# The eight sample rows of a decoder layer: weight rows taken four blocks at a time instead of two, with new numbers for the planner

## The chip, the cores and the metric

The kernel runs on one core of a Trainium2 chip. The metric is the device time of one execution in microseconds; the median of the runs is given. TensorE (PE) multiplies, VectorE (DVE) and ScalarE (ACT) work element by element, GpSimd (POOL) does small work and issues the DMAs that add to their target, and SyncE (SP) issues nearly all other DMAs.

## The reference

One layer of a decoder, all in float32, for 1024 rows of a prompt and 8 sample rows (one new position for each of 8 sequences). Cut to what matters here:

```
xn = rmsnorm(h) * pre_g
u, v, z_a, x_b, z_b, g_a, g_b = split(xn @ w_in)          # 7 x 1024 columns
y_a = gelu(u) * spatial_mix(layernorm(gelu(v))) * silu(z_a)
y_b = pool_branch(x_b) * silu(z_b)
m   = sigmoid(g_a) * (y_a @ w_pa) + sigmoid(g_b) * (y_b @ w_pb)
h   = h + rmsnorm(m @ w_out) * post_g                      # "out"
e   = p @ w_ple
h   = h + rmsnorm(sigmoid(rmsnorm(h) @ w_pg) * e)          # "gate"
```

Outputs are h for prompt and sample, and the new rows of two caches. The change concerns out and gate, the last two products with 1024 x 1024 weights.

## The kernel before

The work runs in stages, one for each product: embedding and x (to 66 us), v, the gate logits, u and z_a, x_b and z_b, y_a and y_b times their weights (to about 804), out (798 to 886) and gate (886 to 970), then the last norm and stores. Out and gate work on four pairs of 128-row blocks of the prompt. For each pair a Strassen scheme makes seven products (named by the weights they use: B11, B21, B22, T1 to T4); each is twelve matmuls of 128 x 512, since every float32 operand is split into a high and a low part (h and l in the names) and three of the four part products are taken. A product lands in PSUM (`acct`), and ScalarE and VectorE add it into the result.

The 8 sample rows are too few for that. In `sample_steps` (L934) their product goes the other way: the 8 rows, transposed (128 x 8), are the stationary operand, and rows of the weights stream past. A *load* brings two blocks of 128 weight rows (512 KB each; tile `worow` for out, `wgrow` for gate) and a *run* calls `sample_round` (L903), which makes four matmuls into four groups of 32 PSUM partitions of one bank (`sps`). Eight blocks make four rounds for each stage. After the last one `sample_sums` adds the groups, and the sample goes on as the prompt does: `out_finish(S)` (norm, then an adding DMA of 32 KB that puts the input row on `hs`), `gate_norm(S)` (`hn`) and `gate_input(S)` (its transposition through `psst`).

What sets the order: nothing is issued when the code is read. `Planner.take` records each operation with a reckoned duration. TensorE's products form a list of steps, and `at(step, ...)` hangs other work on a step; `OS` and `GS` are the steps in out's list (`oflow`) and gate's (`gflow`) at which Sample's rounds begin, and `TURNS` gives for each pair of the prompt the steps of `out_finish`, `gate_norm` and `gate_input`. `wanted` then works out from the end when each operation is due, and `order` deals out the engines' time by it: `LEAD` is how long before its due time an operation may go, `PATIENCE` (and `HASTE` inside `hasty`) how long after its recorded time it may be passed over, `lands` how long a DMA is reckoned to need after its bytes have moved. The result is one fixed order for each engine and for each DMA queue. All is issued from one line, L369, so the profile is read by the names of tiles.

Of the kernel before, what the change touches and what calls it, by code (L numbers as in the profile page):

```python
# [16 lines left out]
NB = D // P  # L17
# [3 lines left out]
HALF = 512  # L21
# [3 lines left out]
QT = WIDE // 2  # L25
EPS = 1e-6
POOL_BUF = 15
FAST = (1, 1, 0, 1)
SIDES = (0, 1, 0, 1, 0, 0, 0, 0)
EARLY = 40.0  # L30
WE = 2
PUSH = {'norm': -5.0, 'half': 0.0, 'cut': 0.0, 'e': -4.0, 'we': -4.0, 'vw': -5.0, 'p': -1.0}
WARM = 8
HASTE = 8.0
TURNS = ((7, 8, 11), (14, 14, 18), (21, 26, 28), (30, 33, 35))
OS, GS = 5, 12
WINDOWS = (2, 4, 8, 16)
PLE = 256
SLOTS = 46
# [55 lines left out]
class Planner:  # L95
# [5 lines left out]

    SEEN = {"tensor": 0.25, "vector": 0.15, "scalar": 0.20, "gpsimd": 0.20}
    TABLES = {AF.Gelu_apprx_tanh: 1, AF.Sigmoid: 2, AF.Silu: 3}
    LOAD, LEAD, PATIENCE, RATE, SPARE = 14.98, 14.0, 55.8, 0.36, 3
    SPARED = 1.0

    def __init__(self, nc, slots, queues):
# [98 lines left out]
    def take(self, engine, method, args, kwargs):  # L206
        given = [*(("out" if i == 0 else "", a) for i, a in enumerate(args)), *kwargs.items()]
        writes = [a for k, a in given if k in ("out", "accum_out") and a is not None]
        reads = [a for k, a in given if k not in ("out", "accum_out") and hasattr(a, "tensor")]
        if kwargs.get("accum_op") is not None:  # L210
            reads += writes
        name = writes[0].tensor.name
        if engine == "tensor" and self.open is not None and self.open[0] == name:
            op = self.open[1]
        else:
            op = Op(engine, len(self.ops), self.clock, self.fixed)
            op.patience, op.push = self.patience, self.push
            self.ops.append(op)
        self.open = (name, op) if engine == "tensor" else None
        op.calls.append((method, args, kwargs))  # L220
        op.spent.append(op.busy)
        if method == "dma_start":
            run = min(self.run(a) for a in (writes[0], reads[0]))
            op.busy, op.moved = 1.0 if engine == "gpsimd" else 0.45, writes[0].size() * 4e-6 * (1 + 0.2 / run)
            op.lands = 2.0
            if kwargs.get("accum_op") is not None:
                op.moved, op.lands = 2 * op.moved, 3.5
        else:
            took = self.duration(engine, method, writes[0], reads, kwargs)
            op.busy += took  # L230
            if engine == "tensor" and not self.fixed:
                self.clock += took
            if engine == "scalar":
                op.table = self.TABLES.get(kwargs["func"], 0)
        for ap in reads:
            self.touch(op, ap, False)
        for ap in writes:
            self.touch(op, ap, True)
# [138 lines left out]
def hybrid_step(  # L377
# [14 lines left out]
    plan = Planner(nc, SLOTS, {"acc": 3, "bank": 2})  # L392
# [8 lines left out]
    def slot(name, shape=(P, T), dt=F32):  # L401
        n_name[0] += 1
        name, n = f"{name}_{n_name[0]}", 1
        for d in shape[1:]:
            n *= d
        model = big.rearrange("p b t -> p (b t)")[:, :n].bitcast(dt)
        if len(shape) > 2:
            dims = "abc"[: len(shape) - 1]
            model = model.rearrange(f"p ({' '.join(dims)}) -> p {' '.join(dims)}", **dict(zip(dims, shape[1:])))
        return plan.slot(name, model, lambda i: spool.tile(list(shape), dt, tag=f"slot{i}", name=name, bufs=1))  # L410
# [21 lines left out]
    def dma(out, in_, by=None):  # L432
        (by or nc.sync).dma_start(out=out, in_=in_)
# [14 lines left out]
    nc.gpsimd.memset(mhalf, -0.5)  # L448
    rc = cpool.tile([P, POOL_BUF], F32, tag="rc", name="rc")
    for j in range(POOL_BUF):  # L450
        nc.gpsimd.memset(rc[:, j : j + 1], 1.0 / (j + 1))
# [42 lines left out]
    class Operand:  # L494
# [37 lines left out]
        def at(self, what, k):  # L532
            return [part[:, k % 2, :] for part in self.parts[what, k // 2]]

    class Stored(Operand):


        ROWS = {"B11": ("b", 0, 0), "B21": ("b", 1, 0), "B22": ("b", 1, 1), "T2": ("low", 0, 0),
                "T1": ("low", 0, 1), "T4": ("high", 0, 0), "T3": ("high", 0, 1)}
# [360 lines left out]
                nc.tensor.matmul(ps, hi(k), wl, start=False, stop=False)  # L900
                nc.tensor.matmul(ps, lo(k), wh, start=False, stop=k == w.nk - 1)

    def sample_round(ps, turned, weights, r):  # L903

        plan.apart()
        for q in range(4):
            k, j = r + q // 2, q % 2
            nc.tensor.matmul(ps[32 * q : 32 * q + NS, :], turned[k], weights(k, j),
                             start=r == 0, stop=r == len(turned) - 2)
# [24 lines left out]
    def sample_steps(key, src, steps, turned, finish):  # L934
        rows, ps = {}, []

        def load(r):
            for k in (r, r + 1):
                t = rows[k] = slot(f"{key}row", (P, D))
                dma(t, src[k * P : (k + 1) * P, :])  # L940

        def run(r):
            if not ps:
                ps.append(bank("sps"))
            sample_round(ps[0], turned(), lambda k, j: rows[k][:, j * HALF : (j + 1) * HALF], r)
            if r == NB - 2:
                finish(ps[0])

        for i, r in enumerate(range(0, NB, 2)):
            at(steps[2 * i], lambda r=r: load(r))  # L950
            at(steps[2 * i + 2], lambda r=r: run(r))


    roots = {}
# [64 lines left out]
    turned = dram.tile([SEQ, D], F32, tag="vturned", name="vturned")  # L1019
# [57 lines left out]
    def early_loads():  # L1077
        lnt["w00"] = cpool.tile([P, NB], F32, tag="w00", name="w00")
        dma(lnt["w00"], w_s[:, 0, 0].partition_broadcast(P))
        dma(o_spool[0, :, : POOL_BUF - 1, :], state[:, 1:, :])  # L1080

# [150 lines left out]
    def pool_state():  # L1232
        dma(big[: NS * POOL_BUF, 7, :D], state.rearrange("b r d -> (b r) d"))

    def small_tables():

        for g, w in enumerate(WINDOWS):
            m = masks[g] = small.tile([P, NS], F32, tag="mask", name=f"mask{g}", bufs=NPAIR)
            nc.gpsimd.memset(m, 1.0)
            nc.gpsimd.affine_select(out=m, in_=m, pattern=[[-POOL_BUF, NS]], compare_op=ALU.is_ge,  # L1240
                                    fill=0.0, base=w - 1 - POOL_BUF, channel_multiplier=1)
            nc.gpsimd.affine_select(out=m, in_=m, pattern=[[POOL_BUF, NS]], compare_op=ALU.is_ge,
# [152 lines left out]
    steps = [s for p in vsteps + gasteps for s in p] + every(usteps)  # L1395
# [24 lines left out]
    for n, t in enumerate([NB - 1, *range(NB - 1)]):  # L1420
        s = 5 + 4 * n
# [51 lines left out]
    rows = lambda t: NS if t == S else P  # L1473
# [93 lines left out]
    def hasty(do, ts):  # L1567
        plan.patience = HASTE
        for t in ts:
            do(t)  # L1570
        plan.patience = plan.PATIENCE
# [102 lines left out]
    for i in range(NPAIR):  # L1674
        ts = [2 * i + 1, 2 * i]
        for do, s in zip((out_finish, gate_norm, gate_input), TURNS[i]):
            at((oflow + gflow)[s], lambda do=do, ts=ts: hasty(do, ts))
# [71 lines left out]
    def begin():  # L1749
# [37 lines left out]
        embed(0, 0)  # L1787
        pushed("e", embed_out, 0, 0, FAST[0])
        embed(1, 0)
        pushed("e", embed_out, 1, 0, FAST[1])  # L1790
        vps = bank("vecs")
# [3 lines left out]
        embed(0, 1)  # L1795
        pushed("e", embed_out, 0, 1, FAST[2])
        pushed("half", x_half, 0, (0, 1))
        pushed("cut", xop.cut, "B11")
        pushed("vw", steps[0].prepare)
        embed(1, 1)  # L1800
        pushed("e", embed_out, 1, 1, FAST[3])
        pushed("half", x_half, 0, (2, 3))
# [73 lines left out]
```

## Time and profile before

| | us |
|---|---|
| runs shown: median (lowest to highest of 3) | 981.69 (978.53 to 984.54) |
| the profiled execution: time | 979.92 |
| its span | 978.2 |
| TensorE busy | 965.4 (99% of the span) |
| VectorE busy | 805.7 (82%) |
| ScalarE busy | 495.5 (51%) |
| granted TensorE clock | 0.997 |

A row of the timeline gives start and duration in us, the engine, the operation, output <- inputs by their names, sizes, and in brackets how long the engine had stood idle and who released it. A row of a tile gives durations in ns (lowest, median, highest) and the first and last start. A matmul in float32 takes two passes and leaves two records, so the four matmuls of a round are eight records. Ends of matmuls are modelled; what counts is the distance of their starts. A row of windows has, behind its stretch and length, the busy time and count of PE, PEld (TensorE's loading of weights), DVE, ACT and POOL in turn, the clock, the share of the DMA engines and GB/s.

### The profile page before, as it was taken

To read this page: it belongs to the slowest core of one execution; us is meant where nothing else is said; L and a number is where in the kernel's file an instruction comes from. 1 tells how busy PE (TensorE), PEld (TensorE's weight loads), DVE (VectorE), ACT (ScalarE), POOL (GpSimd) and SP (SyncE) were. 2 spreads that over 40 slices of the span, in tenths; PEclk is the share of its full clock that TensorE was granted. 3 is DMA by queue.
4 is the path that set the end of the run, shared out by engine and by line. 5 is a ranking of instruction groups with operands and counts; after the bars stand their busy time and mean duration, and the time that the engine had idled before them with its cause. 6 is when DMAs were issued, how large, how long until landed. Compare 5 with 4: busy or idle time off the path is not lost. (4 is left out here: it accounts for less than half of the span.)

```text
span 978.2 us, 15914 instructions
## 1 busy us (share of the span) xinstructions
PE 965.4 (99%) x6048; PEld 858.1 (88%) x6048; DVE 805.7 (82%) x1251; ACT 495.5 (51%) x847; POOL 72.8 (7%) x117
## 2 busy tenths in 40 slices
PE   9999999999999999999999999999999999999996
PEld 7889999999999998999999999999999997778775
DVE  7798568978879789887777897698699899779987
ACT  7674346767434544242423343463363273688655
POOL 2200000000000000000010100000000001323212
PEclk9999999999999999999999999999999999999998
DMA  9464654423457787541222266692592385698996
GB/s 347 148 151 88 152 135 148 162 95 116 171 213 275 257 281 238 188 153 54 87 76 93 75 218 244 222 376 91 170 370 87 120 306 177 160 300 296 222 326 209
DMA packets 128505, 185.81 MB, mean 190 GB/s; under 512 B 42150, under 2 KB 85198, under 8 KB 128421
## 3 DMA queue, kind: packets, MB, share of 16 engines
q1 hardware_dynamic: 126093, 176.91, 54.4%
q0 software_dynamic: 2048, 7.37, 4.2%
q8 instruction: 47, 0.77, 0.3%
q10 hardware_dynamic: 288, 0.52, 0.2%
q14 instruction: 29, 0.24, 0.1%
HBM read 129.27 MB, written 55.96 MB: 189 GB/s over the span
## 5 line engine op out<-in xcount | busy, mean ns | idle before, releaser
L369 DVE TENSOR_TENSOR u<-acc,u 128x520 f32<-128x520 f32 (+1 forms) x90 | 62.5, 695 | 29.8 <-PE acc L369 29.8
L369 POOL TENSOR_TENSOR rstd<-ms,mhalf 128x1 f32<-128x1 f32 (+1 forms) x37 | 30.1, 840 | 448.7 <-DVE ms L369 448.0
L369 ACT ACTIVATE u<-acc 128x512 f32<-128x512 f32 x39 | 23.2, 596 | 35.0 <-PE acc L369 32.5
L369 ACT ACTIVATE zbw<-zbs 128x512 fp32r<-128x512 f32 x16 | 10.0, 629 | 31.6 <-DVE zbs L369 25.8
L369 DVE TENSOR_TENSOR big<-big 128x1024 f32<-128x1024 f32 (+4 forms) x20 | 24.7, 1262 | 0.1
L369 POOL COPY big<-xb 128x1 f32<-128x1 f32 x8 | 3.5, 443 | 260.9 <-ACT xb L369 218.0
L369 ACT ACTIVATE big<-mix 128x256 f32<-128x256 f32 x32 | 11.9, 382 | 20.6 <-PE mix L369 19.7
L369 ACT ACTIVATE paw<-pas 128x512 fp32r<-128x512 f32 x16 | 10.1, 630 | 24.0 <-DVE pas L369 20.0
L369 ACT ACTIVATE pbw<-pbs 128x512 fp32r<-128x512 f32 x16 | 10.1, 630 | 22.3 <-DVE pbs L369 17.0
L369 PE MATMUL accm<-qh,wpoolw 128*128 128x260 f32 (+1 forms) x96 | 21.0, 320 | 0.0
L369 DVE TENSOR_TENSOR zbw<-zbs,zbw 128x512 fp32r<-128x512 f32 x16 | 10.9, 689 | 12.0 <-ACT zbw L369 11.9
L369 ACT ACTIVATE gbw<-gbs 128x512 fp32r<-128x512 f32 x16 | 10.1, 630 | 20.9 <-DVE gbs L369 11.7
L369 ACT ACT_TABLE_LOAD x11 | 14.1, 1283 | 7.4 <-PE acc L369 3.6
L369 ACT ACTIVATE junk<-h 128x512 bf16<-128x512 f32 x25 | 15.7, 627 | 3.5 <-DVE h L369 3.0
L369 DVE SCALAR_TENSOR_TENSOR zb<-accm,gvec,zb 128x512 f32<-128x512 f32 (+1 forms) x16 | 12.0, 750 | 6.5 <-PE accm L369 6.4
L369 PEld LDWEIGHTS accm<-qh,wpoolw 128*128 128x128 f32 x96 | 15.6, 189 | 1.9
L369 ACT ACTIVATE u<-acct 128x512 f32<-128x512 f32 x22 | 13.0, 590 | 7.4 <-PE acct L369 5.1
L369 DVE TENSOR_TENSOR paw<-pas,paw 128x512 fp32r<-128x512 f32 x16 | 10.9, 687 | 6.7 <-ACT paw L369 6.7
L369 ACT ACTIVATE mw<-ms 128x512 fp32r<-128x512 f32 x16 | 10.0, 625 | 12.4 <-DVE ms L369 9.7
L369 ACT ACTIVATE xbw<-xbs 128x512 fp32r<-128x512 f32 x16 | 10.0, 626 | 11.7 <-DVE xbs L369 10.0
L369 PE MATMUL mix<-wst,vh 128*128 128x256 f32 x64 | 15.6, 321 | 0.0
L369 ACT ACTIVATE uw<-us 128x512 fp32r<-128x512 f32 x16 | 10.0, 625 | 10.0 <-DVE us L369 5.9
(660 smaller groups left out, 3557.7 us busy)
## 6 DMA issues: line engine op xcount, KB each, us to landing
ga<-ga SPq DMA_DIRECT2D x16, 516.0 KB, 5.9
gb<-gb SPq DMA_DIRECT2D x16, 516.0 KB, 7.2
ya<-za SPq DMA_DIRECT2D x8, 516.0 KB, 4.9
yb<-zb SPq DMA_DIRECT2D x8, 516.0 KB, 2.6
x<-in_x_prompt_dram SPq DMA_DIRECT2D x8, 512.0 KB, 7.3
vraw<-in_w_in_dram SPq DMA_DIRECT2D x8, 512.0 KB, 5.9
e<-e SPq DMA_DIRECT2D x8, 512.0 KB, 5.9
vturned<-v SPq DMA_DIRECT2D x32, 128.0 KB, 3.4
```

Source lines behind the costliest of these rows:

```text
L369: getattr(getattr(self.nc, e), method)(*(self.real(a) for a in args), **{k: self.real(a) for k, a in kwargs.items()})
```

## The change

`ROWS = 4`: a load takes four blocks and a run makes two rounds one after the other, as one piece that the planner can't part. There are two loads and two runs for each stage in place of four and four. Out's runs hang on steps 5 and 9 of `oflow` in place of 7, 9, 11 and 13, gate's on 16 and 20 of `gflow` in place of 14, 16, 18 and 20. With `OS` the sample's `out_finish`, `gate_norm` and `gate_input` come two steps sooner. `TURNS` changes for the first two pairs: `gate_input` of the first goes from step 11 to 8, `gate_norm` of the second from 14 to 17. An adding DMA of under 0.3 MB, of which there is one, `hs`, is reckoned to land in 7.0 us instead of 3.5. `HASTE`, `LEAD` and `PATIENCE` change slightly.

```diff
+ROWS = 4
-HASTE = 8.0
-TURNS = ((7, 8, 11), (14, 14, 18), (21, 26, 28), (30, 33, 35))
-OS, GS = 5, 12
+HASTE = 7.8
+TURNS = ((7, 8, 8), (14, 17, 18), (21, 26, 28), (30, 33, 35))
+OS, GS = 3, 14
...
-    LOAD, LEAD, PATIENCE, RATE, SPARE = 14.98, 14.0, 55.8, 0.36, 3
+    LOAD, LEAD, PATIENCE, RATE, SPARE = 14.98, 13.58, 51.894, 0.36, 3
...
-                op.moved, op.lands = 2 * op.moved, 3.5
+                op.moved, op.lands = 2 * op.moved, 3.5 if op.moved > 0.3 else 7.0
...
-    def sample_round(ps, turned, weights, r):
-        plan.apart()
+    def sample_round(ps, turned, weights, r, apart=True):
+        if apart:
+            plan.apart()
...
-            for k in (r, r + 1):
+            for k in range(r, r + ROWS):
...
-            sample_round(ps[0], turned(), lambda k, j: rows[k][:, j * HALF : (j + 1) * HALF], r)
-            if r == NB - 2:
+            at_once = turned()
+            for s in range(r, r + ROWS, 2):
+                sample_round(ps[0], at_once, lambda k, j: rows[k][:, j * HALF : (j + 1) * HALF], s, s == r)
+            if r == NB - ROWS:
                 finish(ps[0])
-        for i, r in enumerate(range(0, NB, 2)):
-            at(steps[2 * i], lambda r=r: load(r))
-            at(steps[2 * i + 2], lambda r=r: run(r))
+        for i, r in enumerate(range(0, NB, ROWS)):
+            at(steps[ROWS * i], lambda r=r: load(r))
+            at(steps[ROWS * i + 2], lambda r=r: run(r))
```

The change moves instructions on all engines. Three places on which the prediction rests:

TensorE in out, around Sample's first run; `mw` is the prompt's operand, `big` holds the sample rows. Before:

```order
L369 MATMUL acct_491<-woB22l_8784,mw_8780 128x512
L369 MATMUL acct_491<-woB22h_8724,mw_8780 128x512
L369 MATMUL sps_497<-worow_8709,big 8x512 x2
L369 MATMUL sps_497<-worow_8713,big 8x512 x2
L369 MATMUL acct_502<-woT2h_8546,mw_8814 128x512
L369 MATMUL acct_502<-woT2l_8598,mw_8814 128x512
```

With the change:

```order
L370 MATMUL acct_491<-woT1h_8696,mw_8710 128x512
L370 MATMUL sps_494<-worow_8650,big 8x512 x2
L370 MATMUL sps_494<-worow_8654,big 8x512 x2
L370 MATMUL sps_494<-worow_8661,big 8x512 x2
L370 MATMUL sps_494<-worow_8669,big 8x512 x2
L370 MATMUL acct_491<-woB22h_8715,mw_8786 128x512
L370 MATMUL acct_491<-woB22l_8800,mw_8786 128x512
```

Two rounds stand in a row, and ahead of products (B22, then B11) that in before came ahead of the first round. TensorE's order up to out is the same as in before.

VectorE in the stage of x_b and z_b, near 378 us; `za` is copied out of PSUM (`acc`) in two pieces, `big` is the layer norm of v. Before:

```order
L369 TENSOR_TENSOR xbw_4437<-xbraw_4374,xbw_4437 128x512
L369 TENSOR_TENSOR za_4457<-acc_354,u_4305 128x512
L369 TENSOR_TENSOR xbw_4451<-xbs_4440,xbw_4451 128x512
L369 TENSOR_TENSOR za_4457<-acc_355,u_4305 128x520
L369 SCALAR_TENSOR_TENSOR big<-big,lncol,off_2206 128x8x128 x2
L369 TENSOR_TENSOR za_4457<-za_4457,u_4244 128x1032
```

With the change:

```order
L370 TENSOR_TENSOR xbw_4437<-xbraw_4374,xbw_4437 128x512
L370 SCALAR_TENSOR_TENSOR big<-big,lncol,off_2206 128x8x128
L370 TENSOR_TENSOR xbw_4457<-xbs_4440,xbw_4457 128x512
L370 TENSOR_TENSOR za_4484<-acc_355,u_4305 128x520
L370 TENSOR_TENSOR za_4484<-acc_354,u_4305 128x512
L370 SCALAR_TENSOR_TENSOR big<-big,lncol,off_2206 128x8x128
L370 TENSOR_TENSOR xbw_4451<-xbs_4433,xbw_4451 128x512
```

One of the two instructions on `big` now stands ahead of the 520-wide `za`, and the 512-wide one behind it.

VectorE at the very end of gate, the last norms of the last pair (`ge`; the multiplication by `rstd` is each row's last step before its store). Before:

```order
L369 TENSOR_SCALAR sofar_638<-ssq_635,sofar_636 128x1
L369 TENSOR_TENSOR ge_10078<-ge_10078,out_9456 128x256
L369 SCALAR_TENSOR_TENSOR ge_10058<-ge_10058,rstd_634,hback_10053 128x512
L369 TENSOR_SCALAR ms_639<-ssq_637,sofar_638 128x1
L369 TENSOR_TENSOR ge_10078<-ge_10078,out_9456 128x256
L369 SCALAR_TENSOR_TENSOR ge_10058<-ge_10058,rstd_634,hback_10053 128x512
L369 SCALAR_TENSOR_TENSOR ge_10078<-ge_10078,rstd_640,hback_10060 128x512 x2
```

With the change:

```order
L370 TENSOR_SCALAR ms_633<-ssq_631,sofar_632 128x1
L370 TENSOR_TENSOR ge_10056<-ge_10056,out_9460 128x512
L370 TENSOR_SCALAR sofar_638<-ssq_635,sofar_636 128x1
L370 TENSOR_TENSOR ge_10077<-ge_10077,out_9460 128x256
L370 TENSOR_SCALAR ms_639<-ssq_637,sofar_638 128x1
L370 TENSOR_TENSOR ge_10077<-ge_10077,out_9460 128x256
L370 SCALAR_TENSOR_TENSOR ge_10056<-ge_10056,rstd_634,hback_10051 128x512 x2
L370 SCALAR_TENSOR_TENSOR ge_10077<-ge_10077,rstd_640,hback_10058 128x512 x2
```

The four final multiplications stand together at the end; in before one of them came ahead of `ms_639`. On ScalarE the wide sum of squares that `ms_633` needs now stands behind both 256-wide pieces of `ge`, in before between them.

## The prediction

> **What bounds the kernel now.** I read the page first, then the waits of PE, then the stretches around each edit.
>
> ```profile
> span 978.2 us, 15914 instructions
> PE 965.4 (99%) x6048; PEld 858.1 (88%) x6048; DVE 805.7 (82%) x1251; ACT 495.5 (51%) x847; POOL 72.8 (7%) x117
> ```
>
> TensorE is busy for 99% of the span. A change can only shorten what TensorE executes, remove one of its few stalls, or alter what follows its last matmul. These are the stalls inside the run (time waited, number, longest):
>
> ```profile
> PE acct L369 <- ACT h L369: 1.2, 1, 1.2
> PE acc L369 <- DVE za L369: 0.7, 1, 0.7
> PE acct L369 <- ACT ge L369: 0.6, 1, 0.6
> ```
>
> There is about 3 us to win from stalls, and about as much to lose wherever something is now late. So each term below is around 1 us, against a time of 980. All terms are differences against the profiled execution: 979.92 us, span 978.2.
>
> **Merged rounds.** The change removes no matmul: Sample's rows are still multiplied in eight rounds, four in out and four in gate, eight records each. It removes boundaries between these rounds and the products of 128 columns. One round of before, in TensorE's timeline:
>
> ```profile
> 925.14 0.40 PE L369 MATMUL acct<-wgB11h,hw 128*128 128x512 f32 x1
> ...
> 927.70 0.40 PE L369 MATMUL acct<-wgB11h,hw 128*128 128x512 f32 x1
> 928.03 1.04 PE L369 MATMUL sps<-wgrow,sst 128*8 128x512 f32 x8
> 929.00 0.50 PE L369 MATMUL acct<-wgT2h,hw 128*128 128x512 f32 x1
> 929.34 0.40 PE L369 MATMUL acct<-wgT2l,hw 128*128 128x512 f32 x1
> ```
>
> From 925.14 to 927.70 stand eleven steps of a product, 0.233 us each, so a product of twelve takes 2.8. From 927.70 to 929.34 the round costs 1.64 − 2 × 0.233 = 1.18 us. Inside a round the four column groups run together and each takes two passes. The first and the last start of the four out rounds give the distance of the passes:
>
> ```profile
> L369 PE MATMUL sps<-worow,big x32: 592/594/597, 823.7 to 844.3; 128*8 128x512 f32 x32
> 843.87 1.04 PE L369 MATMUL sps<-worow,big 128*8 128x512 f32 x8
> 844.84 0.50 PE L369 MATMUL acct<-woB11h,mw 128*128 128x512 f32 x1
> ```
>
> The last round starts at 843.87 and its last record at 844.3: 0.43 a pass. A second round straight behind the first should add two passes, 0.87 us, instead of 1.18, a gain of 0.31. There are four such merges (two in out, two in gate): **−1.2 us**. No row shows two rounds back to back. The low bound is no gain, if the second round waits for the first as a product does; the high one is 4 × (1.18 − 0.59), each second round costing one record's length: −2.4. I take the pass distance, the nearest row.
>
> The Trainium skill (TensorEngine Tiling (Array Packing), Key Properties) says that changing the tiling mode drains TensorE, while changing only the tile does not. The trace agrees that the change of mode costs: 927.70 to 928.03 is 0.33 and 929.00 to 929.34 is 0.34, each 0.10 over a step. By that rule alone the eight crossings saved are worth 0.8 us and the sum below would be 0.4 higher.
>
> **The stall at 864.** TensorE stands still once in out:
>
> ```profile
> 864.17 0.39 PE L369 MATMUL acct<-woT4h,mw 128*128 128x512 f32 x1
> 865.74 0.50 PE L369 MATMUL acct<-woB11h,mw 128*128 128x512 f32 x1 [1.18 <-ACT h L369]
> ```
>
> 1.57 less a step is 1.34 us lost. ScalarE was late, for this reason (its timeline, then the group of tile hs):
>
> ```profile
> 862.67 1.06 ACT L369 ACTIVATE hn<-hs 8x1024 f32<-8x1024 f32 x1 [1.73 <-DMA hs<-in_x_sample_dram]
> ...
> 865.10 0.59 ACT L369 ACTIVATE h<-acct 128x512 f32<-128x512 f32 x1
> ```
> ```profile
> L369 ACT ACTIVATE hs<-sps x1: 588/588/588, 846.7 to 846.7; 8x512 f32<-8x512 f32 x1
> ...
> L369 POOL DMA_DIRECT2D hs<-in_x_sample_dram x1: 851/851/851, 856.3 to 856.3; - x1
> ...
> DMA to landing us min/median/max: 6.3/6.3/6.3
> ```
>
> Behind hn stand a junk on h, a junk on acct and the h copy that frees the PSUM of the next product, 865.10 + 0.59. The adding load took 6.3 us where the planner reckoned 3.5; it now reckons 7.0. The new steps matter more. The first group of rounds now follows directly on T1, two products earlier than 823.7, so at 818.1. Four products later, at 818.1 + 2 × 1.02 + 4 × 2.8 = 831.3, comes the second, which ends near 833.4 instead of 844.84. Everything behind it (hs 846.7, the load 856.3, the landing 862.6) moves some 11 us forward: landing near 851. The transposition of hn on TensorE moves forward about ten, and keeps some 2 us behind hn. So the wait goes: **−1.3 us**; bounds 0 (another wait of the same size) and −1.3. The loads for the first group carry no waits on engines and landed from 808 to 816 in before; I cost them at nothing, covered by the product of T1.
>
> **A wait that grows, at 378.** Planner's numbers also move instructions far from Sample. At one place VectorE sets TensorE's next product:
>
> ```profile
> 375.18 0.69 DVE L369 TENSOR_TENSOR xbs<-xbraw,xbraw 128x512 f32<-128x512 f32 x1 [1.89 <-DMA xbraw<-in_w_in_dram]
> ...
> 377.12 0.68 DVE L369 TENSOR_TENSOR za<-acc,u 128x512 f32<-128x512 f32 x1
> 377.72 0.68 DVE L369 TENSOR_TENSOR xbw<-xbs,xbw 128x512 fp32r<-128x512 f32 x1
> 378.32 0.69 DVE L369 TENSOR_TENSOR za<-acc,u 128x520 f32<-128x520 f32 x1
> 378.93 2.47 DVE L369 SCALAR_TENSOR_TENSOR big<-big,lncol,off 128x1024 f32<-128x1024 f32 x2
> ```
> ```profile
> 377.93 0.39 PE L369 MATMUL acc<-xB11h,xbw 128*128 128x512 f32 x1
> 379.06 0.51 PE L369 MATMUL acc<-xB22h,zaw 128*128 128x260 f32 x2 [0.75 <-DVE za L369]
> ```
>
> TensorE starts at 379.06, when the 520-wide za ends (378.32 + 0.69). The order after puts one of the two big instructions (2.47 / 2 = 1.2) ahead of it and the 512-wide za (0.6) behind it. VectorE cannot start sooner, since the xbraw load releases it at 375.18. So za ends, and TensorE starts, 0.6 later: **+0.6 us**, bounds 0 (if that load lands earlier) and +1.2.
>
> **The gate stage.** The four wgrow loads of the first group now stand ahead of the transposing hblocks loads in SP's queue; in before two of them did. Another block's hblocks, which stood there too, go out earlier in return. What hangs on it:
>
> ```profile
> 916.56 3.04 SPq L369 DMA_DIRECT2D hblocks<-h  x4
> ```
> ```profile
> hblocks<-h SPq DMA_DIRECT2D x4, 128.0 KB, 10.1
> ```
> ```profile
> 929.88 1.24 DVE L369 STREAM_TRANSPOSE big<-hblocks 128x1024 f32<-128x1024 f32 x1
> 931.05 0.65 DVE L369 TENSOR_TENSOR hw<-hs,hw 128x512 fp32r<-128x512 f32 x1
> ```
> ```profile
> 932.33 0.63 PE L369 MATMUL acct<-wgT3h,hw 128*128 128x512 f32 x2
> ```
>
> The issues end at 919.6 and the loads take some 10 us to land, so the last is there near 929.1; VectorE needs 2.6 us more (hw ready at 931.7), 0.6 before its use. After, this product comes 3.1 us sooner: 1.3 and 0.6 from out, and one round of 1.2 that stood before it. So the wait begins with a landing after 926.6. The queue ahead has four hblocks less (512 KB in small pieces) and two wgrow more (1 MB in large ones), which I take to be about as long, and starts some 2 us sooner: landing near 927, a wait of **+0.4 us**. Bounds: 0, and rival (b).
>
> The new TURNS record the same norms and transposing loads of the prompt at other steps (gate_input of the first pair three steps sooner, gate_norm of the second three later). They add no instruction; I cost them at nothing, covered by the time in which VectorE idles before 868, and rival (a) is what they cost without that cover.
>
> **The tail.** After the last matmul, in before:
>
> ```profile
> 968.70 0.63 ACT L369 ACTIVATE junk<-ge 128x512 bf16<-128x512 f32 x1 [0.34 <-DVE ge L369]
> ...
> 969.46 0.21 DVE L369 TENSOR_SCALAR ms<-ssq,sofar 128x1 f32<-128x1 f32 x1 [0.52 <-ACT junk L369]
> ...
> 969.78 0.47 ACT L369 ACTIVATE ge<-acct,hscales 128x256 f32<-128x256 f32 x1 [0.36 <-PE acct L369]
> ...
> 972.12 0.66 POOL L369 TENSOR_TENSOR rstd<-ms,mhalf 128x1 f32<-128x1 f32 x1 [1.44 <-DVE ms L369]
> 972.28 2.07 DVE L369 SCALAR_TENSOR_TENSOR ge<-ge,rstd,hback 128x512 f32<-128x512 f32 x3
> ```
>
> The wide junk ran while ScalarE waited for the last product. In the new order it follows both 256-wide ge, so it starts at 970.25, and ms behind it near 971.1. All four final multiplies (2.07 / 3 = 0.69 each) then stand in a row at the end; before, one of them was done by 971.9. They start near 972.6 and end at 972.6 + 2.7 = 975.3, against 974.35: **+0.95 us**, bounds +0.4 (one multiply hidden in POOL's delay) and +1.5.
>
> **Sum.** −1.2 − 1.3 + 0.6 + 0.4 + 0.95 = −0.55, or 979.4 us for the profiled execution. The runs shown have a median of 981.69, 1.77 above it, so I forecast **981.1 us**: no change that can be measured (1%, or 9.8 us, is about what a measurement of this kernel can tell from none).
>
> **Rivals.** (a) *Given back to VectorE.* Through gate it is nearly full:
>
> ```profile
> 860.00:868.00 8.00, 6.82 (x30) 5.26 (x29) 2.47 (x7) 6.16 (x16) 1.65 (x3) 1.00 0.97 254
> 868.00:916.00 48.00, 48.00 (x213) 38.65 (x212) 47.21 (x71) 39.80 (x72) 13.70 (x10) 1.00 0.89 274
> 916.00:932.00 16.00, 16.00 (x74) 12.09 (x73) 13.73 (x24) 11.82 (x26) 5.29 (x6) 1.00 1.04 279
> ```
>
> VectorE (third pair) is busy 47.2 of 48 us from 868 to 916. If it can't start that work sooner, what TensorE gained in out (1.9) is waited out there: −0.55 + 1.9, so 983.0. Against it: VectorE used 2.5 of the 8 us before, idle on the same late hn.
>
> (b) *The loads come too late; slower.* DMA is full from 916 on (share 1.04, 279 GB/s). Two more wgrow ahead of hblocks are 1.05 MB, 3.8 us. If the four hblocks that go out earlier buy nothing, the last lands at 929.1 + 3.8 − 2 = 930.9, hw is ready 2.6 later at 933.5, and its use, due at 932.3 − 3.1 = 929.2, waits 4.3. The time is 981.1 − 0.4 + 4.3 = 985.0; if the second group's last two wgrow are late by as much (3.8), 988.8. It decides from a landing after 926.6.
>
> For this rival speaks the Trainium skill (DMA: Bandwidth & Descriptors, Queues, rings and completion order): on each engine a ring's descriptors are consumed in order. The 10 us to landing above, for 128 KB, agrees with waiting behind others.
>
> (c) *All gain, no loss*: the waits at 378, in gate and the tail are hidden: −2.5, so 979.2. Against it stands the order of the tail, which leaves little to hide behind.
>
> (d) *The merge does nothing*: a second round costs 1.18 too. +0.65, so 982.3.
>
> **Chances.** Forecast 0.45, (a) 0.18, (b) 0.17, (c) 0.15, (d) 0.05. None reaches 1%, save the far end of (b) if both its waits double: slower 0.04; faster by 1% would need more than all stalls of TensorE, 0.02, for what no row shows. Same: 0.94. From (c) less the spread of the three runs (−3) to (b) with its first wait and 1 us more: the range is 976.5 to 986.
>
> **What would show it.** Right: TensorE's waits without acct <- ACT h; eight records of sps followed by eight more within about 0.9 us, no acct between; hs landing near 851; the wait on za at 378 near 1.4; the last multiplies four in a row, about 5 us behind the last ge from acct. Wrong: a wait of acct on hw or of sps on wgrow above 1 us, a new wait of the size of that at 864, or time lost before 800 other than at 378.

## The result, and the profile after

The changed kernel takes 988.79 us (median of 14 runs, 982.72 to 996.32), the kernel before 980.92 in 14 runs on the same chip: a ratio of 1.0087, with a 95% interval from 1.0065 to 1.0109. It is slower by 0.9%. That is within the 1% that the prediction called no change, but 2.8 us above the upper end of its range. The profiled execution takes 987.99 us with a span of 986.3, against 979.92 and 978.2. The runs of the changed kernel spread over 13.6 us, those of before over 6.0, so one trace stands for one of them and not for all.

First the stretches of the three last stages, cut at the first matmul of out, the first of gate and the first 256-wide matmul of gate's last product (972.85 and 965.90). The columns are those of the prediction's table of windows. After:

```profile
797.56:883.01 85.45, 85.45 (x402) 66.95 (x401) 73.42 (x117) 58.83 (x115) 15.43 (x19) 1.00 0.75 217
883.01:972.85 89.84, 82.15 (x357) 62.70 (x356) 72.30 (x121) 55.45 (x113) 21.26 (x21) 0.96 0.80 244
972.85:986.30 13.45, 3.26 (x25) 2.84 (x23) 8.40 (x18) 3.18 (x9) 1.83 (x3) 0.70 0.69 230
```

Before, cut at the same instructions:

```profile
798.49:886.06 87.57, 86.39 (x402) 66.68 (x401) 74.84 (x119) 59.72 (x117) 16.21 (x19) 1.00 0.76 222
886.06:965.90 79.84, 79.84 (x357) 61.02 (x356) 71.62 (x120) 54.72 (x111) 23.80 (x21) 1.00 0.89 261
965.90:978.20 12.30, 3.27 (x25) 2.85 (x23) 7.92 (x18) 3.30 (x9) 1.59 (x2) 0.72 0.71 260
```

Second column: out is 2.12 us shorter, gate 10.00 longer, the end 1.15 longer, and out begins 0.93 earlier; −0.93 − 2.12 + 10.00 + 1.15 = 8.1, the whole difference of the spans. The lengths hold more: in gate TensorE is busy for 82.15 of 89.84 us after, where it was busy for all of it, and the mean clock there (the column behind POOL) is 0.96 instead of 1.00. So nearly all was lost in one stage, by standing still and by running slowly. TensorE's waits after (us in total, times, longest):

```profile
PE acct L370 <- DVE ge L370: 6.8, 1, 6.8
...
PE acct L370 <- ACT u L370: 0.9, 1, 0.9
PE acct L370 <- ACT ge L370: 0.7, 1, 0.7
```

The wait on ACT h of before is gone, and so is that on DVE za. A new one of 6.8 us stands in gate. TensorE's timeline there:

```profile
928.80 0.40 PE L370 MATMUL acct<-wgT2h,hw 128*128 128x512 f32 x1
935.99 0.77 PE L370 MATMUL acct<-wgT3h,hw 128*128 128x512 f32 x1 [6.79 <-DVE ge L370]
936.55 0.63 PE L370 MATMUL acct<-wgT3l,hw 128*128 128x512 f32 x1
...
940.77 0.40 PE L370 MATMUL acct<-wgT3h,hw 128*128 128x512 f32 x1
```

The product T3 of the third pair should have started a step after 928.80, at 929.03, and started at 935.99: 6.96 us lost. VectorE in the same stretch:

```profile
926.69 0.21 DVE L370 TENSOR_SCALAR sofar<-ssq 128x1 f32<-128x1 f32 x2
933.42 1.25 DVE L370 STREAM_TRANSPOSE big<-hblocks 128x1024 f32<-128x1024 f32 x1 [6.52 <-DMA hblocks<-h]
934.59 0.65 DVE L370 TENSOR_TENSOR hw<-hs,hw 128x512 fp32r<-128x512 f32 x1
935.16 0.68 DVE L370 TENSOR_TENSOR ge<-acct,u 128x512 f32<-128x512 f32 x1
```

This is to be read from the bottom. T3 needs the `ge` at 935.16, which frees its PSUM, and the `hw` at 934.59, the low part of its operand. Neither needs anything of `hblocks`: what feeds them was done by 927.7. They stand behind a STREAM_TRANSPOSE for the next pair in VectorE's fixed order, and that waited 6.52 us for four loads. SP's timeline and then a piece of the chain of waits show these loads:

```profile
915.33 0.80 SPq L370 DMA_DIRECT2D wgrow<-wg  x2
917.81 1.79 SPq L370 DMA_DIRECT2D hblocks<-h  x4
```
```profile
916.54 1.25 DVE big L370
...
917.83 0.30 SPq L370
...
919.17 14.13 DMA hblocks<-h
```

The last of the four was issued at 919.17 and landed at 933.30, after 14.1 us, where the same load of before took 10.1. Ahead of it in the queue four wgrow (512 KB each) had gone out where in before there were two. It was issued no sooner than in before, where the last start of these four is at 919.3: in the chain SP's issue follows VectorE's transposition of the group before (916.54).

### The profile page after: what moved, and what is told of

The parts are those of the page before. It is cut to its first block, busy times and chain, and to the rows that moved or that the text cites. A ratio compares the mean times of both kernels' runs of the same rounds, so it can differ in the third digit from the quotient of the medians.

```text
span 986.3 us, 15922 instructions
## 1 busy us (share of the span) xinstructions
PE 966.6 (98%) x6048; PEld 860.1 (87%) x6048; DVE 806.8 (82%) x1251; ACT 496.2 (50%) x847; POOL 64.7 (7%) x117
## 4 chain that ended last, share of the span: by engine, by line
PE 92%; DMA 3%; DVE 3%; ACT 1%; issue 1%; SPq 0%; POOL 0%; DVEq 0%; ACTq 0%; POOLq 0%
PE acc L370 73%; PE acct L370 10%; DMA hblocks<-h 3%; PE e L370 2%; PE accm L370 2%; PE mix L370 1%; PE sps L370 1%; DVE ge L370 1%; PE pst L370 1%; SPq L370 0%; ACT junk L370 0%; DVE big L370 0%; PE warm L370 0%; DVE wgT3l L370 0%; DVE wgT2l L370 0%
## 5 line engine op out<-in xcount | busy, mean ns | idle before, releaser
L370 ACT ACTIVATE zbw<-zbs 128x512 fp32r<-128x512 f32 x16 | 10.1, 629 | 37.2 <-DVE zbs L370 16.3
L370 ACT ACTIVATE pbw<-pbs 128x512 fp32r<-128x512 f32 x16 | 10.1, 630 | 26.1 <-DVE pbs L370 19.2
L370 ACT ACTIVATE gbw<-gbs 128x512 fp32r<-128x512 f32 x16 | 10.1, 630 | 20.1 <-DVE gbs L370 15.2
L370 PE MATMUL acct<-wgT3h,hw 128*128 128x512 f32 x32 | 12.3, 448 | 6.8 <-DVE ge L370 6.8
L370 ACT ACTIVATE u<-acct 128x512 f32<-128x512 f32 x22 | 12.9, 589 | 11.4 <-PE acct L370 6.8
L370 ACT ACTIVATE gbw<-gbraw 128x512 fp32r<-128x512 f32 x12 | 7.4, 628 | 20.9 <-DMA gbraw<-in_w_in_dram 13.1
L370 DVE STREAM_TRANSPOSE big<-hblocks 128x1024 f32<-128x1024 f32 x8 | 9.9, 1239 | 9.3 <-DMA hblocks<-h 9.3
L370 ACT ACT_TABLE_LOAD x11 | 14.1, 1283 | 5.8 <-PE acc L370 2.0
L370 ACT ACTIVATE hw<-hs 128x512 fp32r<-128x512 f32 x16 | 9.9, 624 | 12.6 <-DVE big L370 7.0
L370 ACT ACTIVATE uw<-us 128x512 fp32r<-128x512 f32 x16 | 10.0, 626 | 11.8 <-DVE us L370 7.4
```

Of the source, the lines that this page charges most:

```text
L370: getattr(getattr(self.nc, e), method)(*(self.real(a) for a in args), **{k: self.real(a) for k, a in kwargs.items()})
```

## The experiments

Nearly every kernel below is the changed kernel (one of them the kernel before) with a helper put between the planner and the issue: `play` goes through `self.late()` (`self.less()` where something is left out), which takes the finished order and moves rows in it. So the planner's decisions elsewhere stay as they are. In the diffs `line` is this order and `name` (or `nm`) gives the tile that a row writes; `...` stands for lines that are not shown, and those that only set up these names are left out. Ratios are to the kernel before, run in the same call. The theory was the chain just read: four wgrow ahead make hblocks land late, the transposition waits, and hw, ge and T3 wait behind it.

**The transposition put two instructions later on VectorE.**

```diff
+        k = [i for i, (e, c) in enumerate(line) if e == "vector" and c[0] == "transpose"][-2]
+        late = line.pop(k)
+        behind = [i for i, (e, c) in enumerate(line) if e == "vector" and i >= k][1]
+        line.insert(behind + 1, late)
...
```

> The changed kernel with one move on VectorE alone: the STREAM_TRANSPOSE of hblocks that stood idle until 933.42 now comes behind hw and ge (2 instructions), which the waiting T3 product needs and which need nothing of hblocks. Theory (VectorE's fixed order holds T3 back): T3 starts near 929.1 without a wait instead of 935.99, no slow matmuls (0.43 apart) behind it; T1's low hw still stands behind the transposition, so with a landing at 933.3 a wait of 1 to 2 us remains at T1; time 980 to 982 against 988.8. Rival (the late landing costs the same wherever it is waited for): the wait of some 7 us moves to T1 or B21, time above 985.

Measured: 988.43 us, ratio 1.0077 (1.0049 to 1.0104); a tie with the change as it is. VectorE, then TensorE:

```profile
928.09 0.68 DVE L370 TENSOR_TENSOR ge<-acct,u 128x512 f32<-128x512 f32 x1
934.28 1.25 DVE L370 STREAM_TRANSPOSE big<-hblocks 128x1024 f32<-128x1024 f32 x1 [5.51 <-DMA hblocks<-h]
```
```profile
929.29 0.39 PE L370 MATMUL acct<-wgT3h,hw 128*128 128x512 f32 x1
...
938.37 0.50 PE L370 MATMUL acct<-wgT1h,hw 128*128 128x512 f32 x1 [4.30 <-ACT u L370]
```

ge is done before the transposition and T3 starts at 929.29 without a wait. So T3's wait was one of order, as the theory says. But the loads still land late (934.2), what follows on VectorE is late with them, and the next product, T1, waits 4.3. Moving the waiting instruction moved the wait one product on and won nothing that can be measured: the total follows the landing, as the rival said.

**The second two wgrow put behind hblocks on SP**, alone and with the move above.

```diff
+        rows = [i for i, (e, c) in enumerate(line) if e == "sync"]
+        put = [i for i in rows if "wgrow" in name(line[i][1])][2:4]
+        behind = [i for i in rows if "hblocks" in name(line[i][1]) and i > put[1]][3]
+        line[behind + 1:behind + 1] = [line[i] for i in put]
+        for i in reversed(put):
+            line.pop(i)
...
```

> The changed kernel with one move on SP's queue alone: the second two of the four wgrow loads are issued behind the four hblocks loads instead of ahead of them. Theory (the 1 MB in front of hblocks is what makes it late): hblocks lands some 3 to 4 us sooner, near 929.5 instead of 933.3, T3's wait falls from 7 to about 3 us with fewer slow matmuls; sps then may wait up to 2 us for wgrow; time 983 to 985. Rival (the queue in front is not the reason, but the adding DMAs of GpSimd beside it or the late issue at 917.8): landing stays at 932 or later and the time within 2 us of 988.8.

> Both moves of the two runs before. Theory (order on VectorE decides, the queue adds): T3 and T1 start without a wait on VectorE, perhaps 1 to 2 us on wgrow at the first group of rounds; time 979 to 981, not slower than the kernel before (980.9). Rival (the landing costs the same wherever it is waited for): 984 or more.

Measured: 983.92, ratio 1.0035 (1.0018 to 1.0052), and with both moves 982.05, ratio 1.0019 (1.0005 to 1.0032). Of the 8 us about 5 and 6.5 come back. In the first of them the four loads (the view of DMAs, for the stretch in which they are issued, 927 to 929.6 in this trace):

```profile
hblocks<-h SPq DMA_DIRECT2D x4, 128.0 KB, 6.2
```

and with both moves:

```profile
hblocks<-h SPq DMA_DIRECT2D x4, 128.0 KB, 5.5
```

They take some 6 us instead of 14.1, and T3 waits in neither trace. The profiled execution of the first was the longest of its runs (span 988.5), for waits elsewhere: 2.8 us on za at the place near 378 of which the prediction spoke, 2.3 on wehi and 2.4 in gate's first pair. What is said of its time rests on its twelve runs.

**The second two wgrow left out altogether.** The first group's rounds use blocks 0 and 1 twice, so Sample's product in gate lacks blocks 2 and 3.

```diff
+        rows = [i for i, (e, c) in enumerate(line) if e == "sync" and "wgrow" in name(c)]
+        told = [name(line[i][1]) for i in rows[:4]]
+        swap = {told[2]: told[0], told[3]: told[1]}
...
+        for i in reversed(rows[2:4]):
+            line.pop(i)
```

**GpSimd's first two adding DMAs of ge left out.** Each of them adds h to one block of 128 rows, so two blocks of the output lack h (the expectation below says four). These DMAs (512 KB each) go by another queue and run while hblocks is under way.

```diff
+        adds = [i for i, (e, c) in enumerate(line) if e == "gpsimd" and c[2].get("accum_op") is not None and "ge_" in name(c)]
+        for i in reversed(adds[:2]):
+            line.pop(i)
```

> The changed kernel without the second two wgrow loads of gate's first group: these two rounds read the first two blocks again, so the sample's gate is computed with blocks 2 and 3 left out. All orders else are the same. Theory (1 MB in front): hblocks lands at 929.5 or sooner and T3's wait falls to 3 us or less; time 981 to 984. Rival (something else makes hblocks late): landing after 932, time within 2 us of 988.8.

> The changed kernel without GpSimd's first two adding DMAs of ge (issued at 920.56 and 923.99 in the profile of the change), so four blocks of the output lack h; all other orders are the same. Question: why did 1 MB ahead of hblocks cost some 7 us of its landing and not the 3.8 us of its bytes? Theory: hblocks, pushed back, then shares the DMA engines with the two adding loads. Without them hblocks lands near 929 to 930, T3's wait falls to 2.5 to 3.5 us, time 982 to 985. Rival (the ring alone is that slow): landing at 932 or later, time 987 or more.

Measured: without the two wgrow 982.36, ratio 1.0012 (0.9996 to 1.0027); without the adding DMAs 985.37, ratio 1.0049 (1.0033 to 1.0065). The four hblocks without the two wgrow:

```profile
hblocks<-h SPq DMA_DIRECT2D x4, 128.0 KB, 5.0
```

without the adding DMAs, with all four wgrow ahead (T3 waits 1.1 us in this trace):

```profile
hblocks<-h SPq DMA_DIRECT2D x4, 128.0 KB, 8.3
```

and in the change, with all of them:

```profile
hblocks<-h SPq DMA_DIRECT2D x4, 128.0 KB, 14.1
```

So the 1 MB ahead is worth some 9 us of the 14.1 while the adding DMAs run, and the adding DMAs some 5.8 while the 1 MB is ahead. The two can't be added up, since no run leaves out both: with the wgrow gone the adding DMAs still run, and 5.0 holds, so they cost little unless hblocks has been pushed back into them. Each of these is one trace. With all of them in place the four loads took 11.8 to 14.9 in the traces of other experiments, and the trace without the adding DMAs is of the fastest of ten runs (981.37, their median is 985.37), so its 8.3 may be low. The kernel before has adding DMAs beside these loads too (one is issued at 918.82), and its 10.1 holds their share. For the stretch from 924 to 928 the trace of the change shows these shares of the engines' time by queue (q0 GpSimd's, q1 SP's; they add to over 100%, so they are read as proportions):

```profile
q0 software_dynamic: 135, 0.53, 72.6%
q1 hardware_dynamic: 319, 0.30, 42.4%
```

The Trainium skill (DMA: Bandwidth & Descriptors, Queues, rings and completion order) says that each DMA engine goes round between the queues that have work, packet by packet, and takes up the work of one queue in order. Both halves agree with these rows: what stands ahead in SP's queue delays hblocks, and what stands in GpSimd's slows it without being ahead.

**Joined rounds in out only.** gate goes back to loads of two blocks and rounds that are apart, from step 12; the planner deals anew, and still puts four wgrow ahead of hblocks.

```diff
-    def sample_steps(key, src, steps, turned, finish):
+    def sample_steps(key, src, steps, turned, finish, ROWS=ROWS):
...
-    sample_steps("wg", kept["wg"], gflow[GS:], lambda: samples["h"], embed_gate_sample)
+    sample_steps("wg", kept["wg"], gflow[12:], lambda: samples["h"], embed_gate_sample, 2)
```

> The changed kernel with four blocks at a time in out alone; gate takes two blocks and one round at a time again, from step 12 as before. The planner draws gate anew, and all four wgrow loads still stand ahead of the same hblocks in SP's queue. Theory (that place in the queue is what costs, not the joined rounds): hblocks lands at 931 or later and VectorE's transposition waits for it, time 985 or more. Rival (the joined rounds of gate cost): time 981 or less.

Measured: 986.40, ratio 1.0055 (1.0033 to 1.0076). The loads took 13.6 us and VectorE's transposition at 932.35 waited 3.21 us for them. The rounds in gate were apart, and most of the loss was there, so that much does not need gate's joined rounds. That the place of the loads makes it is shown only in part: the trace is of the fastest of the six runs (981.59), T3 does not wait in it, and the next product, T1, waits 1.23 us at 934.87.

**The tail's order put back**, on top of both moves: the wide junk on ScalarE ahead of the last ge, and one final multiply ahead of the last ms, as before.

```diff
+        act = [i for i, (e, c) in enumerate(line) if e == "scalar"][-4:]
+        line.insert(act[0], line.pop(act[1]))
+        vec = [i for i, (e, c) in enumerate(line) if e == "vector"]
+        scale = [i for i in vec if line[i][1][0] == "scalar_tensor_tensor"][-4]
+        ms = [i for i in vec if i < scale][-2]
+        line.insert(ms, line.pop(scale))
...
```

> The kernel with both moves (982.05 us) and the end as in before: ScalarE's wide sum of squares between the two 256-wide pieces of ge, and the first of VectorE's four last multiplications ahead of the last ms. Theory (the order of the tail costs 0.9 us): from the last matmul's start to VectorE's end 4.9 us instead of 5.7, time 981.1, level with before (980.7) within 0.5. Rival: another chain ends last and the time stays at 982.

Measured: 983.49, ratio 1.0021 (1.0006 to 1.0036); the same kernel without this edit had 1.0019. The trace shows no gain either. From the last matmul's start (972.78) to VectorE's end (976.54 + 2.07) it is still 5.83 us, against 5.81 in the trace with both moves alone. One multiplication does stand ahead of the last ms again, at 975.41. But the wide junk starts at 972.71, 0.07 ahead of the last matmul's start, where in before it was 0.76 ahead (968.70 and 969.46), because ScalarE stood idle for VectorE's ge. So the old order of these instructions does not bring back the old end: VectorE reaches it later.

**The kernel before with hn later on ScalarE**, behind the two junk and the h copy: this removes the stall at 864 without the change.

```diff
+        hn = [i for i, (e, c) in enumerate(line) if e == "scalar" and "hn" in getattr(c[2].get("out"), "name", "")][0]
+        act = [i for i, (e, c) in enumerate(line) if e == "scalar" and i > hn][:3]
...
+        line[hn:hn] = moved
```

> The kernel before with one move on ScalarE: two sums of squares and the h copy that frees the next product's PSUM now come ahead of hn, which waits for the adding load of hs until 862.67. Theory (that order, not the rounds, made the stall of 1.34 us at 864): the stall is gone, time 979.3 against 980.7, the only faster kernel so far. Rival (hn's transposition or the next product's operand is then late): a stall of over 0.7 us stands nearby, time 980.3 or more.

Measured: 980.14, ratio 0.9988 (0.9973 to 1.0003). The wait on ACT h is gone from the trace; in gate and out two smaller waits stand in it that before did not have (0.61 at 875, 0.47 at 895, both on ACT u). By the ratio the gain is 1.2 us, but the interval touches 1, so it is not shown.

**Two wgT loads put behind hblocks.** Shortly ahead of gate a transposition waits 1.60 us for hblocks at 872.84, behind two wgT loads in SP's queue, and TensorE waits 0.9 at 891, in gate's first pair. The edit moves these two loads behind the four hblocks: on the change alone, and together with both moves and the tail.

```diff
+        block = [i for i in rows if "hblocks" in nm(i)]
+        second = block[12:16]
+        put = [i for i in rows if block[11] < i < second[0]]
...
+        moved = [line[i] for i in put]
+        line[second[3] + 1:second[3] + 1] = moved
...
```

> The changed kernel with that last move alone (two wgT loads behind the next four hblocks). Theory: the wait near 892 goes, the long one at 929 stays, since the order there is as it was: 1 to 3 us less than the change, 986 to 988. Rival: no difference, 988.5 or more.

> The changed kernel with all moves so far (two wgrow behind hblocks, VectorE's transposition two later, the tail as in before) and one more on SP's queue: two wgT loads of 512 KB, issued at 861.4 and 861.8 in the profile of the change, go behind the four hblocks that stood next. Theory (the wait of 1.05 us after 891, 2.5 us and slow matmuls in the profile of the kernel with the tail, is the same thing a second time: hblocks behind weight loads, VectorE's transposition held to 872.8): the transposition no longer waits there, T1 near 892 starts without a wait, time 979 to 981 against 983.5 without this move, not slower than before (980.5). Rival (VectorE is simply full from 868 to 916): a wait of 1 us or more stays near 892, time 982 or more.

Measured: alone 988.68, ratio 1.0080 (1.0061 to 1.0098), so no difference; T3 still waited 4.6 us, and TensorE 1.0 at its place of 891, though the transposition ahead of it came without a wait. With the others 981.63, ratio 1.0014 (0.9998 to 1.0030), a tie with the kernel before. In this one the transposition starts at 871.42 without a wait, as the theory wanted, but TensorE still waits:

```profile
PE acct L370 <- ACT u L370: 2.4, 2, 1.6
```

Once at 891 (0.80) and once at 955 (1.64), both times for ScalarE's copy u of a PSUM bank. So hblocks is not the whole cause at 891. It may add to it: over the traces of the changed kernel and its versions, T1 waits 1.5 to 2.4 us there in the four where this transposition waited 2.2 or more, and 0 to 1.4 in the other eight.

**These two waits attacked by order.** At both places VectorE's addition to acct and ScalarE's copy u, which free the bank, go ahead of work that is needed later (halves of wgB21l and wgB22h; three hw and two junk). The rest is as in the kernel just told.

```diff
+        behind_it("acct_1332_570", [("vector", "wgB21l_1317"), ("scalar", "wgB22h_1327")], 12)
...
+        behind_it("acct_1451_627", [("vector", "hw_1450"), ("scalar", "hw_1454"), ("vector", "hw_1452"), ("vector", "hw_1454")], 20)
```

> The change with all the earlier moves together (second two wgrow behind hblocks, the transposition behind hw and ge, the tail as before, two wgT behind hblocks) and two moves more, for the waits of 0.96 us at 891 and 1.80 us at 955 that were left. At 891 the VectorE instruction that adds u to acct goes ahead of the second half of wgB21l, and ScalarE's copy of that acct to u ahead of the second half of wgB22h; at 955 the same pair goes ahead of three hw on VectorE, and of one hw and two junk on ScalarE. Theory (TensorE waits there for nothing but the order of instructions on VectorE and ScalarE): both waits go, 2.7 us, TensorE waits nowhere in gate, and the kernel takes some 979, a ratio of about 0.998 to before. Rival (the two engines are so full there that what is put back makes another product wait): waits of the same sum a product or two later, 981 to 982, ratio about 1.001.

Measured: 984.82, ratio 1.0036 (1.0022 to 1.0050), some 2 us slower than without by the ratios, though their intervals just overlap. TensorE's waits:

```profile
PE acct L370 <- DVE ge L370: 2.4, 1, 2.4
PE acct L370 <- ACT ge L370: 1.9, 1, 1.9
...
PE acct L370 <- ACT u L370: 1.4, 1, 1.4
```

The rival was right in kind and too mild in size (it said 981 to 982). At 955 the wait is gone, but what was put back made two products further on wait, 2.4 us at 966 and 1.9 near 971 (0.7 in the other traces), more than the 1.64 that was removed. At 891 a wait of 1.4 remains: in this trace ScalarE reaches the u of the product before at 890.62, in the one of the kernel without the edit at 889.00.

**The change once more**, to see whether its first trace is typical. No edit.

> The changed kernel once more, for a second profile. Theory: T3's long wait is there again, with hblocks landing between 930 and 935 and matmuls 0.43 apart behind it; the wait near 892 differs from the first profile's 1.05. Rival (the first profile was a rare one): a landing before 929 and no wait of over 3 us.

Measured: 990.75 us, span 989.0. The four loads took 12.9 us, T3 waits again, and the wait at 891 is longer:

```profile
PE acct L370 <- DVE ge L370: 5.8, 1, 5.8
PE acct L370 <- ACT u L370: 2.9, 2, 2.3
```

## Why the prediction was wrong

The step that failed is in the part on the gate stage: "The queue ahead has four hblocks less (512 KB in small pieces) and two wgrow more (1 MB in large ones), which I take to be about as long, and starts some 2 us sooner: landing near 927, a wait of +0.4 us." The place was right, and so was the chain from landing to transposition to hw to TensorE. The landing was wrong: 933.30. Both halves of the step failed. The loads did not start sooner: the last one was issued at 919.17, against 919.3 in before, though the first wgrow ahead of it went out 2.2 us sooner (912.43 against 914.66). And the queue was not about as long: the landing took 14.1 us instead of 10.1. The experiments with the two wgrow moved and left out show that these two are what made it late (5.0 to 6.2 us without them ahead), so the four hblocks that went out earlier bought little.

Rival (b) held this mechanism, with its deciding point of 926.6, and priced it at a landing of 930.9 and a wait of 4.3. Its 3.8 us for 1 MB were near the 4.0 measured. It was short because it, too, took off 2 us for a sooner start: 929.1 + 3.8 is 932.9. Beyond that came a cost that no part of the prediction had: the matmuls behind the wait are slow. From 935.99 to 940.77 T3 takes 4.78 us for eleven steps, where eleven of 0.233 are 2.56: 2.2 us on top of the 6.96. That the far end of rival (b), 988.8, is the measured median is luck: it counted on a second wait, for wgrow, and TensorE waits for no wgrow in the trace.

The terms one by one, in the profiled execution:

- **Gate stage:** predicted +0.4. The stage is 10.00 us longer with two merges in it that save 0.66. So 10.66 was lost: 6.96 by T3's start, 2.2 by the slow matmuls behind it, 1.05 by a wait at 891 (1.28 between two starts there, less a step); about 0.45 is spread. The wait at 891 falls in a term that the prediction put at nothing, the transposing loads at other steps: in before this transposition came at 869.89 without a wait, after at 872.84. How much of the 1.05 is due to it is open.
- **Merged rounds:** predicted −1.2, and right by its own working. One run of both rounds, after:

```profile
816.87 0.40 PE L370 MATMUL acct<-woT1h,mw 128*128 128x512 f32 x1
817.20 1.90 PE L370 MATMUL sps<-worow,big 128*8 128x512 f32 x16
819.03 0.50 PE L370 MATMUL acct<-woB22h,mw 128*128 128x512 f32 x1
819.37 0.39 PE L370 MATMUL acct<-woB22l,mw 128*128 128x512 f32 x1
```

  From 816.87 to 819.37 is 2.50, less two steps 2.03, where two rounds apart cost 2 × 1.18 = 2.36. That is 0.33 each against 0.31, and 1.3 for the four. Sixteen records run through without a break. The value of 0.8 that stood beside it, by the changes of mode alone, was too low.
- **The stall at 864:** predicted −1.3, and right. ACT h is no longer among the waits. The sample's adding load was expected to land near 851. It is issued at 843.2, and hn, which needs it, starts at 850.6 (the tile hs):

```profile
L370 POOL DMA_DIRECT2D hs<-in_x_sample_dram x1: 853/853/853, 843.2 to 843.2; - x1
...
L370 ACT ACTIVATE hn<-hs x1: 1043/1043/1043, 850.6 to 850.6; 8x1024 f32<-8x1024 f32 x1
```

  Out is 2.12 shorter: 1.34 for this and 0.66 for two merges, and 0.1 open.
- **The wait at 378:** predicted +0.6; in this trace the wait is gone instead, 0.9 less. VectorE, after:

```profile
372.83 0.69 DVE L370 TENSOR_TENSOR xbs<-xbraw,xbraw 128x512 f32<-128x512 f32 x1 [0.30 <-DMA xbraw<-in_w_in_dram]
...
374.77 1.28 DVE L370 SCALAR_TENSOR_TENSOR big<-big,lncol,off 128x1024 f32<-128x1024 f32 x1
375.97 0.68 DVE L370 TENSOR_TENSOR xbw<-xbs,xbw 128x512 fp32r<-128x512 f32 x1
376.57 1.29 DVE L370 TENSOR_TENSOR za<-acc,u 128x520 f32<-128x520 f32 x2
```

  The order is the one foretold, big ahead of za. But xbraw released VectorE at 372.83 instead of 375.18. The prediction had named this case ("if that load lands earlier"), as a bound of 0; it gave 0.9 back. In other runs of the same order the wait on za was 2.8 (wgrow behind), 1.0 (both moves) and 0 (the change again). Why it differs from run to run stays open; taking one row of a landing as fixed was a mistake.
- **The tail:** predicted +0.95. From the last matmul's start to VectorE's end it is 979.65 + 2.73 − 976.57 = 5.81 after, and 974.35 − 969.46 = 4.89 before, where the last matmul started at 969.46: +0.92. The four multiplies stand in a row as predicted:

```profile
976.57 0.28 PE L370 MATMUL acct<-wgB22h,hw 128*128 128x256 f32 x1
...
979.65 2.73 DVE L370 SCALAR_TENSOR_TENSOR ge<-ge,rstd,hback 128x512 f32<-128x512 f32 x4
```

  So size and order came out. But with the old order put back it stays 5.83, so the order alone does not explain the 0.92, and that the size came out is in part luck. In the change VectorE comes late to the end: two multiplications of the sample's ge and a wait of 0.46 for GpSimd's rstd stand at 973 to 975 between what feeds it, where in before both multiplications were done by 966.1. That these are the cause is not shown.
- **From the profile to the median:** the forecast added 1.77 us, from three runs. Fourteen runs have 980.92, so 1.0. That is small beside the rest.

The gains of out (2.0) and the merges of gate (0.66) do not show as a faster kernel, even with the late loads mended. In the kernel with all these moves two waits of 0.80 and 1.64 remain in gate, and the attempt to take them away by order brought others. It looks as if VectorE and ScalarE had no slack there to take what TensorE gained. This is rival (a) at a second place, and argued rather than shown: no run gave VectorE less to do. No version here beats the kernel before by more than can be measured; the kernel before with hn later (0.9988) comes nearest.

## What to carry to other kernels

When an edit enlarges the loads ahead of a small urgent one, price the small one's landing with everything that will be in flight beside it, on other queues too: here the small loads took 5.0 us with adding DMAs beside them, 8.3 behind 1 MB more, and 14.1 with both. Look then in the waiting engine's order for what stands behind the waiting instruction and does not need the data; but moving the instruction alone helps only if the work behind it has slack as well. And give a long wait of TensorE a price beyond its length: here seven of eight waits of 2.3 us or more had one.

## What the runs showed of the hardware

After a long wait TensorE ran at half speed for a while. The change's stretches from 928 to 936 and from 936 to 940 (the clock is the value before the last two):

```profile
928.00:936.00 8.00, 1.21 (x7) 0.67 (x5) 2.58 (x4) 0.75 (x2) 0.00 (x0) 0.87 0.34 67
936.00:940.00 4.00, 4.00 (x10) 3.13 (x11) 4.00 (x8) 3.26 (x7) 0.56 (x1) 0.50 0.62 201
```

The granted clock is 0.50 there, and matmuls start 0.427 us apart instead of 0.233. How long a wait it takes is not one number. Over all traces, waits of up to 2.14 us between two starts in gate were never followed by slow matmuls. Of eight between 2.64 and 7.19, seven were. The slow stretch need not begin with the restart: in the kernel with both moves and the tail TensorE waited at 891,

```profile
891.87 0.39 PE L370 MATMUL acct<-wgT3h,hw 128*128 128x512 f32 x1
894.64 0.50 PE L370 MATMUL acct<-wgT1h,hw 128*128 128x512 f32 x1 [2.38 <-ACT u L370]
894.98 0.51 PE L370 MATMUL acct<-wgT1l,hw 128*128 128x512 f32 x1
895.29 1.05 PE L370 MATMUL acct<-wgT1h,hw 128*128 128x512 f32 x2
...
898.63 0.40 PE L370 MATMUL acct<-wgT1l,hw 128*128 128x512 f32 x1
```

and the slow spacing runs from 895.29 to 898.63, 3.34 us that begin 3.4 after the last start ahead of the wait (about 4 in the two other traces with a wait of this length). The exception, in the last experiment, is a wait of 2.44 before 965.93, after which the clock stays whole:

```profile
966.00:970.00 4.00, 4.00 (x23) 3.49 (x24) 3.73 (x9) 3.31 (x9) 1.98 (x1) 1.00 1.06 242
```

The Trainium skill (TensorE: Matmul & The Clock Gate, The HAM clock gate) says that the clock is halved after an idle window of about 3.4 us, and that these windows run freely and are not reset when a kernel starts. The length of the slow stretch and its late beginning agree with that, and so does that one wait of this length was spared. That a wait must fill a whole window does not agree: 2.3 to 2.4 us between busy matmuls was enough in three traces. The runs do not settle where the windows lie.
